# A second, transposed layout of the input for the first projection, with the normalisation moved

## The chip, the cores and the metric

The kernel runs on one core of one Trainium2 chip. The metric is the device time of one execution in microseconds (us); the median of a few runs is given. TensorE (PE in the profile) multiplies matrices into PSUM, VectorE (DVE) and ScalarE (ACT) do elementwise work from SBUF and PSUM, GpSimd (POOL) does elementwise work from SBUF and issues DMAs, SyncE (SP) issues DMAs. Each engine runs its own instructions in order and waits on semaphores for the others.

## The reference, cut to what matters

Two layers over 2048 tokens of width 1024: a Mamba-2 mixer and a latent attention mixer, each behind an RMS norm, and a last RMS norm. The part at issue is the first norm and the first projection:

```python
def rms_norm(x, g):
    y = xf * lax.rsqrt(jnp.mean(xf * xf, axis=-1, keepdims=True) + EPS)
    return y * g

hn = rms_norm(h, g_pre[0])                 # h is x, (2048, 1024)
proj = hn @ ssm_w_in                       # (1024, 5152)
z, xBC, dt_raw = split(proj)               # 2048, 3072, 32 columns
xBC = silu(causal_depthwise_conv(xBC, conv_w, conv_b))   # width 4, along the tokens
dt = softplus(dt_raw + dt_bias)
y = ssd_chunked_scan(...)                  # scan over 32 heads
y = group_norm(y * silu(z)) @ ssm_w_out    # added to the residual stream
```

The norm's factor r = rsqrt(mean(x^2) + EPS) is one number for each token. It may therefore be multiplied in before the projection or, since the projection is linear, on its result.

## The kernel before

Float32 accuracy is kept with pairs: each operand of a product is split into a rounded half (`hi`, by ScalarE) and the remainder (`lo`, by VectorE; `split`, lines 102 to 109), and each product is three matmuls (`mm3`, lines 80 to 84).

Layer 0 goes by blocks of 512 tokens (b = 0 to 3) and within a block by four groups of 8 heads (g). For each (b, g) there are these steps:

- `xbc` (line 283): B and C (two tiles of 128 channels) and then x (four tiles) of a group, channels on partitions, 512 tokens along the free axis; weights from `wunit`, loaded by SP and split. `evacuate` copies the PSUM bank to `craw` (ScalarE, L311), and makes the convolution (ScalarE L315, three times VectorE L317), tanh and product (L319, L320). `craw` has three buffers, PSUM's `mm` four.
- `zgate` (line 326): the gate z with tokens on partitions; `evacuate` takes tanh (L340) and a product (L341) straight from PSUM.
- `ssd` (line 438): the scan over four chunks of 128 tokens; GpSimd makes the remainders of some operands (`halves`, L455).
- `outp` (line 347): the output projection of the group, added to the residual rows `hs`.

Before a block's first group come `load_x` (line 255), which loads 512 rows of x, takes the mean square of each (ScalarE Square with accumulation, L155), the factor (`rsqrt`, a chain of ten small VectorE operations, lines 131 to 148) and multiplies the rows by it (L269); `prep` (line 271), which transposes the rows with 32 TensorE transposes of 128x128 (L163) into PSUM and splits them with the gain g0 into the eight tiles `xT` (L108 ScalarE, L109 VectorE; eight buffers, so a block's tiles take the places of the block before); and `steps` (line 375), the step sizes: 16 matmuls with `wdt` (L382), whose weights are split once at the start, then softplus on VectorE, then L422 to L424, whose result goes to DRAM (`cumT`) and comes back broadcast over the partitions (L471).

`mamba` (line 215) sets the order. Ahead of everything stand the first block's `load_x`, the constants, `prep`, `steps`, `xbc` and `zgate` of (0, 0). Then, item by item, the scan of (b, g) is woven with the output projection of the item before and the `xbc` and `zgate` of the next one; in group 2 of a block `load_x` of the next block is called at once, and `prep` and `steps` of it come last in the weave:

```python
            if g == G - 2 and b + 1 < NB:
                self.load_x(b + 1, self.a["x"][(b + 1) * TB:(b + 2) * TB])
                parts += [self.prep(b + 1, self.g0), self.steps(b + 1)]
```

The final order on each engine's queue is made by a scheduler from this order, priorities and its own estimates; tiles are places in pools with a fixed number of buffers, and a tile's first writer waits for the last reader of what lay there. After layer 0 come the second layer's projections (`mla`), attention and the output, which use `load_x` and `prep` too and are not changed.

Of the kernel before, what the change touches and what calls it, by code (L numbers as in the profile page):

```python
# [9 lines left out]
F32 = mybir.dt.float32  # L10
# [55 lines left out]
class Net:  # L66
# [50 lines left out]
    def wunit(self, src, n, scale=None, late=False):  # L117
        """Split weights; in the last layer's gates they take the place of the scan's states."""
# [12 lines left out]
    def rsqrt(self, pool, ms, n):  # L131
        """(ms + EPS) ** -0.5, elementwise on [P, n]."""
# [17 lines left out]
    def rows_rms(self, tiles, junk, width):  # L150
        """rsqrt(mean(x^2) + EPS) of each of the [P, width] tiles -> [P, len]."""
# [7 lines left out]
    def transposed(self, tiles, k, tag="tr"):  # L159
        """[P, k-th 128 columns] of four token tiles -> one PSUM bank [128 columns, 512 tokens]."""  # L160
        ps = self.t(self.pp, tag, [P, TB], bufs=4)
        for i, x in enumerate(tiles):
            self.nc.tensor.transpose(ps[:, i * P:(i + 1) * P], x[:, k * P:(k + 1) * P], self.ident)  # L163
        return ps

# [1 line left out]
    def constants(self, cp):  # L167
# [3 lines left out]
        # [lower triangle | hidden]  # L171
# [6 lines left out]
    def layer_constants(self, cp):  # L178
# [3 lines left out]
        wdt = self.t(self.wp, "wraw", [P, TB], bufs=WRAW)  # L182
        nc.sync.dma_start(wdt[:, :KD * H].rearrange("p (k c) -> p k c", k=KD),
                          a["ssm_w_in"][:, DI + 3072:].rearrange("(k p) c -> p k c", p=P))
# [7 lines left out]
        self.wdt = cp.tile([P, KD, 2, H], F32R, name="wdt")  # L192
        self.split(self.wdt[:, :, 0], self.wdt[:, :, 1], wdt[:, :KD * H].rearrange("p (k c) -> p k c", k=KD))
# [7 lines left out]
    # ---- layer 0: Mamba-2, by blocks of 512 tokens and groups of 8 heads;  # L201
# [13 lines left out]
    def mamba(self, cp):  # L215
        nc = self.nc
        self.state = [None] * G
# [36 lines left out]

    def load_x(self, b, src, tag="hx"):
        """A block's rows, normalised."""
# [14 lines left out]
    def prep(self, b, gain=None, tag="tr", each=4):  # L271
        """The normalised rows, channels on partitions, split."""
# [10 lines left out]
    def xbc(self, b, g):  # L283
        """B, C and x of a group: channels on partitions, convolution along the free axis, SiLU."""
        nc, w_in, xT = self.nc, self.a["ssm_w_in"], self.xT[b]
        outs = []
        for chans, tag, bufs in (([16 + g, 20 + g], "BC", 4), ([4 * g + j for j in range(4)], "xs", 8)):
# [19 lines left out]
            def evacuate(bank, i):  # L307
# [4 lines left out]
                nc.gpsimd.tensor_copy(self.halo[:, ch, :], raw[:, TB:TB + 3])  # L312
                acc = self.t(self.sp, "cacc", [P, TB], bufs=2)
                wk = [self.cw[:, 4 * ch + k:4 * ch + k + 1] for k in range(4)]
                nc.scalar.activation(acc, raw[:, 0:TB], AF.Identity, scale=wk[0], bias=self.cb[:, ch:ch + 1])  # L315
                for k in range(1, 4):
                    nc.vector.scalar_tensor_tensor(acc, raw[:, k:k + TB], wk[k], acc, ALU.mult, ALU.add)  # L317
                o = self.t(self.sp, tag, [P, TB], bufs=bufs)
                nc.scalar.activation(o, acc, AF.Tanh)  # L319
# [839 lines left out]
```

## Time and profile before

| | us |
|---|---|
| median of 3 runs | 3246.47 |
| lowest and highest run | 3245.31, 3246.8 |
| span of the profiled execution, first to last instruction | 3243.9 |
| TensorE busy in the span | 3194.4 |
| VectorE busy | 2589.0 |
| ScalarE busy | 2049.7 |
| GpSimd busy | 641.7 |

The profiled execution has no time of its own in the list of runs beside its span; what lies around the span is read from the difference to the median, 2.6 us. In the profile's rows L12 is line 12 of the kernel; a group's row has engine, operation, tiles written and read, sizes and count; a timeline row begins with the start and the duration; a row of the waits has the waiting instruction, what ended its wait, the sum, the count and the longest; a row of the stretches has the stretch, its length and the busy time of TensorE, the weight loads, VectorE, ScalarE and GpSimd, with instruction counts, then TensorE's granted clock, the share of the DMA engines and GB/s.

### The profile page before, as it was taken

To read this page: it belongs to the slowest core of one execution; us is meant where nothing else is said; L and a number is where in the kernel's file an instruction comes from. 1 tells how busy PE (TensorE), PEld (TensorE's weight loads), DVE (VectorE), ACT (ScalarE), POOL (GpSimd) and SP (SyncE) were. 2 spreads that over 40 slices of the span, in tenths; PEclk is the share of its full clock that TensorE was granted. 3 is DMA by queue.
4 is the path that set the end of the run, shared out by engine and by line. 5 is a ranking of instruction groups with operands and counts; after the bars stand their busy time and mean duration, and the time that the engine had idled before them with its cause. 6 is when DMAs were issued, how large, how long until landed. Compare 5 with 4: busy or idle time off the path is not lost. (4 is left out here: it accounts for less than half of the span.)

```text
span 3243.9 us, 50420 instructions
## 1 busy us (share of the span) xinstructions
PE 3194.4 (98%) x16704; PEld 2651.4 (82%) x16704; DVE 2589.0 (80%) x5480; ACT 2049.7 (63%) x5113; POOL 641.7 (20%) x854
## 2 busy tenths in 40 slices
PE   8999999999999999999999999999999999999998
PEld 6788888888888888888878888878888888887787
DVE  6888888888889888888777665678888888888665
ACT  5666666656657666666655554477777777777522
POOL 1221122221222212221111211322222222223100
PEclk9999999999999999999999999999999999999999
DMA  5333334333433344333476766954544445454385
GB/s 174 105 99 95 118 122 131 101 91 123 143 95 103 96 125 140 104 96 116 126 271 230 250 218 192 291 114 86 100 88 93 93 85 104 87 106 110 93 271 161
DMA packets 241397, 433.57 MB, mean 134 GB/s; under 512 B 26192, under 2 KB 100688, under 8 KB 239696
## 3 DMA queue, kind: packets, MB, share of 16 engines
q1 hardware_dynamic: 166704, 289.28, 29.4%
q0 software_dynamic: 74432, 141.06, 18.0%
q8 instruction: 132, 2.16, 0.3%
q14 instruction: 129, 1.06, 0.1%
HBM read 328.67 MB, written 101.58 MB: 133 GB/s over the span
## 5 line engine op out<-in xcount | busy, mean ns | idle before, releaser
L106 DVE TENSOR_TENSOR PTs<-tr,PTs 128x512 fp32r<-128x512 f32 (+2 forms) x576 | 359.9, 643 | 109.1 <-ACT PTs L105 106.4
L105 ACT ACTIVATE PTs<-tr 128x512 fp32r<-128x512 f32 (+2 forms) x576 | 314.2, 571 | 153.7 <-PE tr L901 152.4
L886 ACT ACTIVATE Pr<-mm,nm 128x512 f32<-128x512 f32 (+2 forms) x631 | 397.4, 641 | 20.2 <-DVE nm L878 20.2
L874 DVE TENSOR_REDUCE mx<-mm 128x1 f32<-128x512 f32 (+2 forms) x631 | 375.5, 608 | 33.0 <-PE mm L84 28.4
L105 ACT ACTIVATE wsp<-wraw 128x512 fp32r<-128x512 f32 (+1 forms) x452 | 251.8, 574 | 175.8 <-PE mm L84 88.4
L106 DVE TENSOR_TENSOR wsp<-wraw,wsp 128x512 fp32r<-128x512 f32 (+1 forms) x452 | 300.5, 678 | 70.0 <-ACT wsp L105 69.7
L82 PE MATMUL mm<-xT,wsp 128*128 128x512 f32 x800 | 324.4, 405 | 0.0
L901 PE MATMUL tr<-pack,Pr 128*128 128x128 f32 x2176 | 317.9, 273 | 2.6 <-ACT Os L923 2.4
L83 PE MATMUL mm<-xT,wsp 128*128 128x512 f32 x800 | 316.5, 396 | 0.0
L84 PE MATMUL mm<-xT,wsp 128*128 128x512 f32 x800 | 316.1, 395 | 0.0
L901 PEld LDWEIGHTS tr<-pack,Pr 128*128 128x128 f32 x2176 | 254.3, 141 | 40.9 <-ACT Os L923 2.9
L82 PE MATMUL mm<-K,xT 96*128 96x512 f32 (+2 forms) x639 | 248.6, 389 | 6.6 <-ACT Pr L886 5.2
L916 PE MATMUL tr<-PTs,xT 128*128 128x512 f32 (+2 forms) x576 | 253.9, 441 | 0.1
L82 PE MATMUL mm<-wsp,xT 128*128 128x512 f32 (+1 forms) x640 | 244.4, 382 | 0.0
L83 PE MATMUL mm<-wsp,xT 128*128 128x512 f32 (+1 forms) x640 | 240.0, 375 | 0.0
L84 PE MATMUL mm<-wsp,xT 128*128 128x512 f32 (+1 forms) x640 | 239.2, 375 | 0.0
L84 PE MATMUL mm<-K,xT 96*128 96x512 f32 (+2 forms) x639 | 231.5, 362 | 0.0
L317 DVE SCALAR_TENSOR_TENSOR cacc<-craw,pack,cacc 128x512 f32<-128x512 f32 x288 | 216.7, 774 | 18.4 <-ACT cacc L315 17.8
L83 PE MATMUL mm<-K,xT 96*128 96x512 f32 (+2 forms) x639 | 231.4, 362 | 0.0
L455 POOL TENSOR_TENSOR Xp<-Xw,Xp 128x512 fp32r<-128x512 f32 x64 | 83.0, 1298 | 708.1 <-ACT Xp L454 399.5
L497 ACT ACTIVATE Xw<-tr,d_wend 128x64 f32<-128x64 f32 x512 | 182.9, 358 | 55.4 <-DVE Xd L493 54.4
L917 PE MATMUL tr<-PTs,xT 128*128 128x512 f32 (+2 forms) x576 | 216.1, 377 | 0.0
(355 smaller groups left out, 8323.9 us busy)
## 6 DMA issues: line engine op xcount, KB each, us to landing
wraw<-in_ssm_w_in_dram SPq DMA_DIRECT2D x256, 256.0 KB, 2.8
big<-cumT SPq DMA_DIRECT2D x64, 512.0 KB, 4.2
wraw<-in_ssm_w_out_dram SPq DMA_DIRECT2D x128, 256.0 KB, 2.6
wraw<-in_ssm_w_in_dram SPq DMA_DIRECT2D x129, 128.0 KB, 2.2
xT<-qn_d POOLq DMA_DIRECT2D x64, 256.0 KB, 4.2
xT<-v_d POOLq DMA_DIRECT2D x32, 512.0 KB, 5.3
K<-kn_d POOLq DMA_DIRECT2D x15, 1024.0 KB, 9.2
wraw<-in_mla_w_uq_dram SPq DMA_DIRECT2D x36, 256.0 KB, 5.5
```

Source lines behind the costliest of these rows:

```text
L82: mm(out, l_hi, r_hi, start=start, stop=False)
L83: mm(out, l_hi, r_lo, start=False, stop=False)
L84: mm(out, l_lo, r_hi, start=False, stop=stop)
L105: nc.scalar.activation(hi, src, AF.Copy)
L106: nc.vector.tensor_tensor(lo, src, hi.bitcast(F32), ALU.subtract)
L317: nc.vector.scalar_tensor_tensor(acc, raw[:, k:k + TB], wk[k], acc, ALU.mult, ALU.add)
L497: act(Xw[:, hc], px[:, hc], AF.Copy, scale=wend[:, h0 + h:h0 + h + 1])
L874: v.tensor_reduce(mx[:, n:n + 1], s[:, :w], AX.X, ALU.max)
L886: nc.scalar.activation(x[:, :w], s[:, :w], AF.Exp, bias=nm, accum_out=sm[:, n:n + 1])
L901: nc.tensor.transpose(pt[:, j * P:(j + 1) * P], st["P"][j][kb], self.ident)
L916: nc.tensor.matmul(st["O"][:, c], vals[h, kb // 8][:, kb % 8, :], u[:, 0], start=kb == 0, stop=False)
L917: nc.tensor.matmul(st["O"][:, c], vals[h, kb // 8][:, kb % 8, :], u[:, 1], start=False, stop=kb == nk - 1)
```

## The change

The host hands the kernel the same input twice, as rows (`x`) and transposed (`xT`). The first projection's tiles are loaded from the transposed layout by SP, so layer 0's `prep`, and with it the transposes, is gone; the rows are still loaded, for r and, in block 0, as the residual rows.

- Block 0: `xT` is split as loaded, without r. The projection runs on it, and r is multiplied in afterwards: on each of the 24 channel tiles ahead of the convolution (VectorE, with r broadcast over the partitions, `rb`), on the 16 gate tiles in a new ScalarE copy (r by partition, `r0`), and on the step projection. The convolutions of the first B and C tiles are put off (`later`). `rb` is made by writing r to DRAM and reading it back broadcast, both from GpSimd's queue.
- Blocks 1 to 3: the rows are loaded early by GpSimd's queue, r is made in `load_xT` and broadcast the same way, and GpSimd multiplies each of the eight loaded tiles by `rb` before it is split. `load_xT` is a generator in the place of `prep`; its Squares are issued where the weave reaches it.
- The step weights are loaded and split anew in each block and use a weight buffer; the first block's `steps` comes after `xbc`.

The rest of the diff removes comments.

```diff
 def layer_constants
-        wdt = self.t(self.wp, "wraw", [P, TB], bufs=WRAW)
...
-        self.split(self.wdt[:, :, 0], self.wdt[:, :, 1], ...)
+        self.r0 = cp.tile([P, 4], F32, name="r0")
 def mamba
-        self.load_x(0, self.a["x"][0:TB])
+        rows, first = self.load_xT(0), self.xbc(0, 0)
+        next(rows)
         self.layer_constants(cp)
-        for part in (self.prep(0, self.g0), self.steps(0), self.xbc(0, 0), self.zgate(0, 0)):
+        for n in range(16):
+            next(rows, None)
+            next(first)
+            if n == 12:
+                while self.later:
+                    self.later.pop(0)()
+        for part in (first, self.steps(0), self.zgate(0, 0)):
...
             if g == G - 2 and b + 1 < NB:
-                self.load_x(b + 1, self.a["x"][(b + 1) * TB:(b + 2) * TB])
-                parts += [self.prep(b + 1, self.g0), self.steps(b + 1)]
+                parts += [self.load_xT(b + 1), self.steps(b + 1)]
+    def load_xT(self, b):
+        nc, v, t0 = self.nc, self.nc.vector, b * TB
+        rows = [self.a["x"][t0 + i * P:t0 + (i + 1) * P, :] for i in range(4)]
+
+        def norm(xs):
+            r = self.rows_rms(xs, [self.t(self.sp, "yt", [P, D], BF16, bufs=2) for _ in xs], D)
+            nc.gpsimd.dma_start(self.r_d[t0:t0 + TB].rearrange("(i p) -> p i", p=P), r)
+            rb = self.rb = self.t(self.hh, "rb", [P, TB], bufs=1)
+            self.behind = nc.gpsimd.dma_start(rb, self.r_d[t0:t0 + TB].partition_broadcast(P))
+            return r
+
+        self.xT[b] = []
+        if b:
+            xs = [self.t(self.hh, "hx", [P, D], bufs=4) for _ in range(4)]
+            with self.tc.issue_after(self.behind.ins):
+                for x, row in zip(xs, rows):
+                    nc.gpsimd.dma_start(x, row)
+            norm(xs)
+        for k in range(KD):
+            if k % 2 == 0:
+                pair = self.t(self.hh, "hx", [P, 2, TB], bufs=4)
+            x = pair[:, k % 2]
+            last = nc.sync.dma_start(x, self.a["xT"][k * P:(k + 1) * P, t0:t0 + TB])
+            if b:
+                nc.gpsimd.tensor_tensor(x, x, self.rb, ALU.mult)
+            elif k == 0:
+                yield
+            u = self.t(self.xq, "xT", [P, 2, TB], F32R, bufs=8)
+            self.split(u[:, 0, :], u[:, 1, :], x, self.g0[:, k:k + 1])
+            self.xT[b].append(u)
+            if k % 4 == 3 or b == 0 and k:
+                yield
+        if b == 0:
+            self.hs[0] = [self.t(self.hh, "hs", [P, D], bufs=4) for _ in range(4)]
+            for x, row in zip(self.hs[0], rows):
+                with self.tc.issue_after(last.ins):
+                    last = nc.sync.dma_start(x, row)
+                yield
+            v.tensor_copy(self.r0, norm(self.hs[0]))
+            yield
 def xbc, evacuate
+                def conv():
+                    if b == 0:
+                        nc.vector.tensor_tensor(raw[:, 3:], raw[:, 3:], self.rb, ALU.mult)
...
+                if b + g == 0 and tag == "BC":
+                    self.later.append(conv)
+                else:
+                    conv()
 def zgate, evacuate
+            if b == 0:
+                zn = self.t(self.sp, "craw", [P, TB], bufs=3)
+                nc.scalar.activation(zn, bank, AF.Copy, scale=self.r0[:, i:i + 1])
+                bank = zn
 def steps
+        raw = self.t(self.wp, "wraw", [P, TB], bufs=WRAW)[:, :KD * H]...
+        nc.sync.dma_start(raw, self.a["ssm_w_in"][:, DI + 3072:]...)
+        w = self.t(self.wp, "wsp", [P, 2, TB], F32R, bufs=WSP)[:, 0]...
+        self.split(w[:, :, 0], w[:, :, 1], raw)
...
-        nc.scalar.activation(rt, ps[0:2 * H, :], AF.Copy)
+        if b:
+            nc.scalar.activation(rt, ps[0:2 * H, :], AF.Copy)
+        else:
+            v.tensor_tensor(rt, ps[0:2 * H, :], self.rb[0:2 * H], ALU.mult)
 def layout
+        "xT": np.asarray(x)[0].T
```

More of the change, by code (lines that the diff above doesn't have):

```diff
@@ L191, in layer_constants @@
         nc.vector.memset(self.mk[:, P:], NEG)
-        self.wdt = cp.tile([P, KD, 2, H], F32R, name="wdt")
-        self.split(self.wdt[:, :, 0], self.wdt[:, :, 1], wdt[:, :KD * H].rearrange("p (k c) -> p k c", k=KD))
         nc.vector.tensor_scalar(self.cw, self.cw, 0.5, None, ALU.mult)
@@ L349, in outp @@
         nc, a, t0 = self.nc, self.a, b * TB
-        if g == 0:
+        if g == 0 and b:
             self.hs[b] = [self.t(self.hh, "hs", [P, D], bufs=4) for _ in range(4)]
@@ L377, in steps @@
         nc, v, xT = self.nc, self.nc.vector, self.xT[b]
+        raw = self.t(self.wp, "wraw", [P, TB], bufs=WRAW)[:, :KD * H].rearrange("p (k c) -> p k c", k=KD)
+        nc.sync.dma_start(raw, self.a["ssm_w_in"][:, DI + 3072:].rearrange("(k p) c -> p k c", p=P))
+        w = self.t(self.wp, "wsp", [P, 2, TB], F32R, bufs=WSP)[:, 0].rearrange("p (k n h) -> p k n h", k=KD, n=2)
+        self.split(w[:, :, 0], w[:, :, 1], raw)
         ps = self.t(self.pp, "tr", [P, TB], bufs=4)
@@ L381, in steps @@
             for n in range(2):
-                nc.tensor.matmul(ps[0:2 * H, :], self.wdt[:, k].rearrange("p n h -> p (n h)"), xT[k][:, n, :],
+                nc.tensor.matmul(ps[0:2 * H, :], w[:, k].rearrange("p n h -> p (n h)"), xT[k][:, n, :],
                                  start=k + n == 0, stop=k + n == KD)
@@ L1093, in run @@
             self.constants(cp)
+            self.r_d = dp.tile([T], F32, name="r_d")
             self.h_d = dp.tile([T, D], F32, name="h_d")
@@ L1131, in layout @@
     out = {
-        "x": np.asarray(x)[0], "positions": np.asarray(positions)[0],
+        "x": np.asarray(x)[0], "xT": np.asarray(x)[0].T, "positions": np.asarray(positions)[0],
         "c_pack": np.concatenate([pack[k] for k, _ in PACKED], axis=1),
```

24 lines of the change are left out of this document (11 added, 13 removed).

## The prediction

> **What bounds the kernel now.** I read the page's busy table first, then TensorE's waits, then the stretches.
>
> ```profile
> span 3243.9 us, 50420 instructions
> ...
> PE 3194.4 (98%) x16704; PEld 2651.4 (82%) x16704; DVE 2589.0 (80%) x5480; ACT 2049.7 (63%) x5113; POOL 641.7 (20%) x854
> ```
> ```profile
> PE tr L163 <- DMA wraw<-in_ssm_w_in_dram: 14.1, 1, 14.1
> ```
> ```profile
> 0.00:22.00 22.00, 7.94 (x39) 7.08 (x40) 11.07 (x43) 14.64 (x28) 0.64 (x7) 1.00 0.72 241
> ...
> 200.00:300.00 100.00, 100.00 (x488) 82.67 (x487) 85.85 (x178) 65.86 (x163) 19.73 (x24) 1.00 0.34 101
> ```
>
> TensorE has work in 98% of the span; 49.5 us are idle, and 14.1 of them are one wait, the start. In layer 0 (the second stretch; its columns are TensorE, weight load, VectorE, ScalarE, GpSimd) TensorE never rests and VectorE is at 86%. So the kernel is as long as TensorE's queue plus its holes: an instruction taken off TensorE is worth its place in the queue, an instruction on VectorE or GpSimd is free until TensorE reaches something that waits for it. The sums below are made on the profiled span, 3243.9 us. The median of the runs, 3246.47, is 2.6 above it for what lies around the span, which I leave alone. About 0.2% (6.5 us) is what a measurement here can tell from no change.
>
> **Removed: the transposes of blocks 1 to 3.** The PE timeline at the turn from block 0 to block 1:
>
> ```profile
> 346.66 0.39 PE L83 MATMUL mm<-wsp,xT 128*128 128x512 f32 x1
> 346.89 0.39 PE L84 MATMUL mm<-wsp,xT 128*128 128x512 f32 x1
> ...
> 351.04 0.60 PE L163 MATMUL tr<-pack,hx 128*128 128x128 f32 x4
> 351.39 0.48 PE L83 MATMUL mm<-wsp,yT 128*128 128x512 f32 x1
> 351.71 0.60 PE L163 MATMUL tr<-pack,hx 128*128 128x128 f32 x4
> ```
>
> One matmul of 512 columns takes 0.23 us of queue (346.66 to 346.89). Four transposes and one matmul take 351.71 - 351.04 = 0.67, so four transposes 0.44. A block has eight such fours, 3.5 us; three blocks 10.5 us. VectorE also loses the scaling of the rows (L269, four of 0.75 us a block, below), off the path. Block 0's 32 transposes are part of the start, next.
>
> **The start.**
>
> ```profile
> 14.06 3.78 PE L163 MATMUL tr<-pack,hx 128*128 128x128 f32 x16 [14.06 <-DMA wraw<-in_ssm_w_in_dram]
> 17.49 0.78 PE L82 MATMUL mm<-xT,wsp 128*128 128x512 f32 x1
> ...
> 21.70 3.87 PE L382 MATMUL tr<-xT,wdt 128*64 128x512 f32 x16
> ```
> ```profile
> 82.35 0.39 PE L82 MATMUL mm<-xT,wsp 128*128 128x512 f32 x1
> ```
> ```profile
> 10.34 0.21 DVE L194 TENSOR_SCALAR pack<-pack 128x96 f32<-128x96 f32 x1 [9.11 <-DMA pack<-in_c_pack_dram]
> ...
> 10.55 0.17 DVE L135 TENSOR_SCALAR rsx<-ms 128x4 f32<-128x4 f32 x1
> ...
> 13.46 0.16 DVE L146 SCALAR_TENSOR_TENSOR rsy<-rsq,rsy 128x4 f32<-128x4 f32 x1
> ```
>
> Today the constants land at 10.3 behind 2 MB of rows, the factor r is ready at 13.6, and the second group's first matmul starts at 82.35. In the changed program's order the constants follow 256 KB of x^T, and the first matmul needs only them, one weight tile and two splits: I put it at 7 us. TensorE starts cold (first matmul 0.78 us, not 0.39), which lasts some 6 us now and will again. From there to the second group it has 240 matmuls of 0.23 (56 us), the 16 step matmuls (3.8), some small ones (1) and about 3 us of cold: 70.8. But the convolutions of block 0 now wait for r in its broadcast form. The rows come after x^T, and two of their Squares stand behind the evacuations of the first two banks, which TensorE fills near 20 and 21 (48 matmuls, the first ones cold): the last Square ends near 24, r, with three weight splits between its links, is there near 29, and the broadcast (8.2 us, below) near 37. VectorE then has eleven operations for B and C before it goes on, and by its order the step chain reaches L486 some 1 to 3 us after TensorE does, with one wait before it (L453) of about 2. That makes 75, and a gain of 7.5 (3 to 11).
>
> **Block 0 behind the projection.**
>
> ```profile
> L320 DVE SCALAR_TENSOR_TENSOR xs<-xs,cacc 128x512 f32<-128x512 f32 x64 | 43.7, 685 | 0.7 <-ACT xs L319 0.7
> ```
>
> 24 channel tiles get one more VectorE multiplication. No row shows it; the nearest, with the same shape and both inputs in SBUF, takes 0.69: 16.4 us, mostly within 270 us where VectorE is 86% busy, so it goes to about 91%. The 16 gate tiles get a ScalarE copy (0.60, as the gate row below), 9.6 us on an engine with a third of its time free. Hidden as long as TensorE's next scan step isn't waiting; I charge 2 us (0 to 5). The step weights, split anew in each block (one 128 KB load, half a microsecond on each of two engines), are placed ahead of need and charged at nothing.
>
> **Blocks 1 to 3: the chain that takes the transposes' place.** This is the part that decides. Let t0 be the start of a block's last gate matmul plus 0.4. The rows of the next block are fetched early, but the changed program places the Squares between the gate evacuations, on ScalarE in this order: evacuation, Square, evacuation, Square.
>
> ```profile
> 347.32 0.60 ACT L340 ACTIVATE sz<-mm 128x512 f32<-128x512 f32 x1
> ```
> ```profile
> L269 DVE TENSOR_SCALAR hx<-hx,rsy x36: 348/747/754, 13.7 to 1793.1; 128x1024 f32<-128x1024 f32 x24, 128x256 f32<-128x256 f32 x12
> L155 ACT ACTIVATE yt<-hx x28: 1039/1042/1072, 4.1 to 1768.0; 128x1024 bf16<-128x1024 f32 x28
> L155 ACT ACTIVATION_READ_ACCUMULATOR yt<-hx x28: 185/186/217, 5.0 to 1769.0; 128x1 f32 x28
> ```
> ```profile
> L108 ACT ACTIVATE xT<-tr,pack x32: 677/688/703, 15.3 to 1141.1; 128x512 fp32r<-128x512 f32 x32
> L109 DVE SCALAR_TENSOR_TENSOR xT<-tr,pack,xT x32: 737/744/753, 16.8 to 1142.2; 128x512 fp32r<-128x512 f32 x32
> ```
> ```profile
> DMA to landing us min/median/max: 1.5/1.7/1.9
> ```
> ```profile
> xT<-qn_d POOLq DMA_DIRECT2D x64, 256.0 KB, 4.2
> ```
> ```profile
> DMA to landing us min/median/max: 2.2/5.6/9.9
> ```
>
> A Square with its read-out is 1.23 us, an evacuation 0.60 (and it starts right at t0 today). Stepping through the order, the last Square ends at t0 + 1.4 (t0 + 4.4 at the first turn, where the extra copies stand between). The r chain took 3.1 us at the start; here five larger VectorE operations of 0.6 to 0.75 stand between its links, so 6 us: r at +7.4 (first turn +9.1, as most of the five are done by then). GpSimd then sends r to DRAM and reads it back over 128 partitions, the second waiting for the first. Neither exists today. The landings above are a 64 KB write from SP (the cumulative decays), a 256 KB read from GpSimd, and everything on kr_d from GpSimd. Ends for the pair: 1.5 + 2.2 = 3.7 and 5.6 + 5.6 = 11.2; I take 4 + 4.2 = 8.2, near the middle, because the write goes out in 512 pieces of 4 bytes, finer than any row. [...]
>
> So the broadcast is there at t0 + 15.6 (+17.3 at the first turn). GpSimd multiplies eight tiles, and each is then split by ScalarE and VectorE:
>
> ```profile
> L455 POOL TENSOR_TENSOR Xp<-Xw,Xp x64: 1263/1296/1576, 90.9 to 1590.7; 128x512 fp32r<-128x512 f32 x64
> ```
> ```profile
> 264.59 1.29 POOL L455 TENSOR_TENSOR Xp<-Xw,Xp 128x512 fp32r<-128x512 f32 x1 [22.43 <-ACT Xp L454]
> ```
> ```profile
> 265.14 1.01 DVE L106 TENSOR_TENSOR wsp<-wraw,wsp 128x256 fp32r<-128x256 f32 x1 [0.25 <-ACT wsp L105]
> ...
> 274.60 0.43 DVE L106 TENSOR_TENSOR wsp<-wraw,wsp 128x256 fp32r<-128x256 f32 x1 [0.43 <-ACT wsp L105]
> ```
>
> Alone a product takes 1.26 to 1.30. But a VectorE split with both inputs in SBUF that meets a GpSimd product waits for its end: the one at 265.14 took 1.01 instead of 0.43 and ran on to 266.15, the product ended at 265.88. Until now these splits read PSUM; now they read the tile from SBUF, and each meets the next product. [...] Taking turns, a tile costs 1.26 + 0.65 = 1.9, and the last split ends 15.4 after the broadcast, at +31.0 (+32.7). Without the contention it would be 8 x 1.26 + 1.4 = 11.5, 3.9 less.
>
> TensorE's order decides what that costs. The step matmuls of the next block, which need these splits, now stand between output-projection matmuls: 52 matmuls and some transposes lie between t0 and the first of them, 24 more up to the last, so TensorE gets there at +18.9 if it never waits (first turn: 60 and 24, with half a microsecond for a weight split, +21.6). The wait is 31.0 - 18.9 = 12.1 at two turns and 32.7 - 21.6 = 11.1 at the first: 35.3 us. Behind it in TensorE's queue stand the rest of the output projection and the scan; VectorE and ScalarE stand in their own queues before the same splits, so weight splits and evacuations wait too; on GpSimd the scan's products are behind the eight and behind four DMAs that wait for the splits. All shift together, so I add nothing for them.
>
> **Sum.** -10.5 (transposes), -7.5 (start), +2 (block 0), +35.3 (waits) = +19.3, on the span 3263, on the median 3265.8; I say 3265.
>
> **Rivals.**
> - *Short chain.* [...] Chance 0.22, of which 0.14 within 0.2%.
> - *Chain hidden: faster.* The last split would have to be there at +18.9. That needs r in broadcast form 12.1 us earlier, before the last gate matmul; it decides from a Square placed about a group ahead, since the rows are there. Then -10.5 - 7.5 + 2 gives 3230. For it: TensorE has no wait at these turns now. Against it: the order of the Squares. Chance 0.10.
> - *Start eaten.* If VectorE's late convolutions of block 0 hold the first scan too, the start gives 0 and block 0 costs 5: 3276. Chance 0.10.
> - *Slow write.* The 4-byte pieces bring the pair to 11.2 or above: +3 a turn and at the start, 3277 and up. Chance 0.13.
>
> **How the numbers follow.** The forecast keeps 0.45, own range 3255 to 3274. Left out are the faster rival (0.10) and most of the slow write (0.10): range 3241 to 3280. Faster by over 0.2% (below 3240): 0.11; within 0.2%: 0.16; slower: 0.73.
>
> **What would show it.** Right: the first matmul near 7 us and the second group near 75; three waits of 10 us or so at the step matmuls, ended by ScalarE or VectorE splits of xT, whose own idle is ended by GpSimd; splits of xT longer than 0.75 us on VectorE. Wrong: PE without idle at the turns, or GpSimd's products ending before TensorE reaches the step matmuls; then the forecast falls to the faster rival.

## The result and the profile after

The changed kernel takes 3329.3 us (median of 4 runs, 3326.2 to 3333.1) where the kernel before takes 3245.9 in the same comparison: ratio 1.0249, 95% interval 1.0236 to 1.0261. It is slower, as forecast, but by 83 us instead of 19. Its profiled execution has a span of 3326.6 us.

The page of the changed kernel first. TensorE has 128 instructions fewer than before and is still busy 18 us longer, and its share falls from 98 to 97%:

```profile
span 3326.6 us, 50286 instructions
...
PE 3212.5 (97%) x16576; PEld 2650.2 (80%) x16576; DVE 2612.3 (79%) x5485; ACT 2060.4 (62%) x5127; POOL 699.5 (21%) x898
```

TensorE's waits in the changed kernel (engine, line, what ended the wait: us in all, times, longest). The first and third line are the step matmuls that wait for the splits of x^T. Of the other two the wait for a weight split (`wsp`) did not exist before, and the wait for y came to 1.0 us:

```profile
PE tr L443 <- ACT xT L108: 26.9, 3, 9.1
PE mm L84 <- DVE wsp L106: 13.2, 4, 4.6
PE tr L443 <- DVE xT L109: 9.2, 13, 0.8
...
PE tr L595 <- DVE y L590: 7.3, 4, 3.2
```

To see where the time went I set the same instruction of both programs side by side: the transposes of y for the third chunk of the last group but one of blocks 0, 1 and 2, shortly ahead of each turn. Before (the first fence) and after (the second), PE timeline:

```profile
323.94 0.60 PE L531 MATMUL tr<-pack,y 128*128 128x128 f32 x4
...
716.26 0.60 PE L531 MATMUL tr<-pack,y 128*128 128x128 f32 x4
...
1111.04 0.60 PE L531 MATMUL tr<-pack,y 128*128 128x128 f32 x4
```
```profile
333.30 0.60 PE L595 MATMUL tr<-pack,y 128*128 128x128 f32 x4
...
751.75 0.60 PE L595 MATMUL tr<-pack,y 128*128 128x128 f32 x4
...
1169.92 0.60 PE L595 MATMUL tr<-pack,y 128*128 128x128 f32 x4
```

The differences are +9.4, +35.5 and +58.9, and +82.7 at the end of the span. So start and block 0 cost 9.4 us (forecast: a gain of 5.5), and the three turns 26.1, 23.4 and 23.8 (forecast: 11.1 or 12.1 less the 3.5 of the transposes). With the 3.5 us of work that each turn saves, TensorE loses 29.6, 26.9 and 27.3 us at a turn. (The third figure holds all that follows, to the end of the span.)

**One turn in the trace.** TensorE at the first turn. Its last gate matmul starts at 356.26 (t0 is 356.7). It has come to the step matmuls at 371.87 and stands there for 8.94 us; the matmuls behind the wait start every 0.43 us instead of every 0.23; the last step matmul starts at 392.95, and three more waits follow within 50 us:

```profile
356.26 0.39 PE L84 MATMUL mm<-wsp,xT 128*128 128x512 f32 x1
...
371.48 0.39 PE L84 MATMUL mm<-wsp,yT 128*128 128x512 f32 x1
380.81 0.69 PE L443 MATMUL tr<-xT,wsp 128*64 128x512 f32 x1 [8.94 <-ACT xT L108]
381.30 0.63 PE L82 MATMUL mm<-wsp,yT 128*128 128x512 f32 x1
381.73 0.63 PE L83 MATMUL mm<-wsp,yT 128*128 128x512 f32 x1
...
392.95 0.44 PE L443 MATMUL tr<-xT,wsp 128*64 128x512 f32 x1
...
403.57 0.51 PE L82 MATMUL mm<-xT,wsp 128*128 128x512 f32 x1 [1.90 <-DVE hs L425]
...
411.72 0.49 PE L486 MATMUL tr<-big,pack 128*128 128x128 f32 x2 [1.61 <-DVE big L484]
...
440.87 2.07 PE L84 MATMUL mm<-xT,wsp 128*128 128x512 f32 x4 [3.90 <-DVE wsp L106]
```

GpSimd at the same turn. It writes r at 365.48, can issue the read only at 375.03, and starts the first product at 378.75:

```profile
365.48 0.80 POOL L265 DMA_DIRECT2D r_d<-rsy  x1 [1.25 <-DVE rss L142]
375.03 0.54 POOL L267 DMA_DIRECT2D rb<-r_d  x1 [8.75 <-DMA r_d<-rsy]
378.75 12.61 POOL L283 TENSOR_TENSOR hx<-hx,rb 128x512 f32<-128x512 f32 x8 [3.17 <-issue]
```

ScalarE's and VectorE's splits behind it come at a pitch of 1.69 us (382.95 to 384.64), and the last one ends at 392.89:

```profile
382.95 0.72 ACT L108 ACTIVATE xT<-hx,pack 128x512 fp32r<-128x512 f32 x1 [0.96 <-POOL hx L283]
384.64 0.72 ACT L108 ACTIVATE xT<-hx,pack 128x512 fp32r<-128x512 f32 x1 [0.96 <-POOL hx L283]
```
```profile
392.14 0.75 DVE L109 SCALAR_TENSOR_TENSOR xT<-hx,pack,xT 128x512 fp32r<-128x512 f32 x1 [0.24 <-ACT xT L108]
```

The same as stretches (their columns are TensorE, weight load, VectorE, ScalarE and GpSimd, then the granted clock). In the first TensorE does 25 instructions, 5.8 us of queue at 0.23, in 21 us; VectorE is half idle. In the second, which begins 42 us after the first ends, TensorE runs short again while VectorE is busy for 86% of the time:

```profile
372.00:393.00 21.00, 9.22 (x25) 4.62 (x25) 10.52 (x9) 6.29 (x10) 14.73 (x12) 0.76 0.15 32
...
435.00:447.00 12.00, 7.76 (x34) 6.72 (x35) 10.35 (x27) 8.29 (x26) 2.09 (x3) 0.74 0.22 67
```

VectorE's queue between the two stretches tells where the second comes from. VectorE stands 4.67 us in the step chain for ScalarE, which itself stands 6.54 us for a weight load (to 400.87). Then it is busy for 36.85 of the 40 us from 401.5 to 441.5. The weight split that TensorE waits 3.90 us for has no wait of its own ahead of it: it stands in that queue behind other work.

```profile
401.52 0.23 DVE L472 TENSOR_SCALAR big<-big 128x128 f32<-128x128 f32 x1 [4.67 <-ACT big L471]
...
440.13 1.28 DVE L106 TENSOR_TENSOR wsp<-wraw,wsp 128x512 fp32r<-128x512 f32 x2
```

A wait also costs beyond itself. In the two stretches above, with the waits of 8.94 and 3.90 us, the granted clock is 0.76 and 0.74, and the matmuls behind each wait start every 0.43 us. Behind the wait of 1.90 at 403.57 they start every 0.23 again; behind one of 1.98 at the second turn (822.02) they do so for 1 us and then start every 0.43 for 3 us. And behind a wait of 3.17 us in block 0, with TensorE busy ahead of it, four transposes take 0.92 instead of 0.60 and the next matmuls start every 0.43 too. So the trace shows no length from which a wait has this price.

```profile
147.10 0.92 PE L595 MATMUL tr<-pack,y 128*128 128x128 f32 x4 [3.17 <-DVE y L590]
```

**The start.** GpSimd, VectorE and TensorE in the changed kernel's first 85 us:

```profile
30.96 0.98 POOL L265 DMA_DIRECT2D r_d<-rsy  x1 [29.37 <-DVE r L297]
40.11 0.57 POOL L267 DMA_DIRECT2D rb<-r_d  x1 [8.16 <-DMA r_d<-rsy]
```
```profile
45.93 1.29 DVE L359 TENSOR_TENSOR craw<-craw,rb 128x512 f32<-128x512 f32 x2 [1.90 <-DMA rb<-r_d]
```
```profile
52.21 0.79 PE L82 MATMUL mm<-wsp,xT 128*128 128x512 f32 x1 [4.22 <-ACT craw L356]
...
61.15 0.69 PE L453 MATMUL tr<-pack,yt 64*128 64x64 f32 x4 [5.49 <-DVE yt L450]
...
84.68 0.39 PE L82 MATMUL mm<-xT,wsp 128*128 128x512 f32 x1
```

r is ready when GpSimd sends it, at 30.96, and lies on all partitions only at 45.9. Evacuations and the step chain wait for it, and TensorE for them, twice. The second group's first matmul starts at 84.68, 2.3 us later than before.

### The profile page after: what moved, and what is told of

It reads as the page before. It is cut to its first block, busy times and chain, and to the rows that moved or that the text cites. A ratio compares the mean times of both kernels' runs of the same rounds, so it can differ in the third digit from the quotient of the medians.

```text
span 3326.6 us, 50286 instructions
## 1 busy us (share of the span) xinstructions
PE 3212.5 (97%) x16576; PEld 2650.2 (80%) x16576; DVE 2612.3 (79%) x5485; ACT 2060.4 (62%) x5127; POOL 699.5 (21%) x898
## 4 chain that ended last, share of the span: by engine, by line
PE 52%; DVE 4%; DMA 3%; ACT 2%; issue 1%; POOL 0%; SPq 0%; ACTq 0%; DVEq 0%; POOLq 0%
PE mm L82 9%; PE mm L84 9%; PE mm L83 9%; PE tr L965 6%; PE tr L980 4%; PE tr L981 4%; PE tr L82 3%; PE tr L84 3%; PE tr L83 3%; DMA os<-ri_d 1%; PE tr L568 1%; DVE cacc L365 1%; DMA wraw<-in_mla_w_in_dram 1%; ACT PTs L105 1%; DMA wraw<-in_kv_w_up_dram 1%
## 5 line engine op out<-in xcount | busy, mean ns | idle before, releaser
L938 DVE TENSOR_REDUCE mx<-mm 128x1 f32<-128x512 f32 (+2 forms) x631 | 375.6, 608 | 35.3 <-PE mm L84 30.4
```

What stands on the lines that cost most here:

```text
L938: v.tensor_reduce(mx[:, n:n + 1], s[:, :w], AX.X, ALU.max)
```

## The experiments

All times stand beside the kernel before, run with them (3246.7 to 3247.9). "Lost" below is worked out from the PE timeline of each kernel: of every gap between two starts, what is over 0.23 us for a matmul of 512 columns (0.115 for 128, 0.107 for 64 columns), summed over a stretch; "up to the last step matmul" begins 25 us before the first of them, "behind" is the 80 us after the last. Overshoots of some 0.1 us, which every kernel has, are left out, so the figures hold to about 1 us; the kernel before loses some 1 us at most on either side.

I began with two theories. A: the chain's end sets the wait, and VectorE, 86% loaded, falls behind by as much and pays behind the turn. B: what stands behind the turn comes from the new order of the queues and not from the wait. The instructions of every engine are laid out anew when a part of the program is moved, so an edit changes more than the place of its own lines.

### One part alone: block 0, and its broadcast

Blocks 1 to 3 as before, block 0 as in the changed kernel (e2):

```
-                parts += [self.load_xT(b + 1), self.steps(b + 1)]
+                self.load_x(b + 1, self.a["x"][(b + 1) * TB:(b + 2) * TB])
+                parts += [self.prep(b + 1, self.g0), self.steps(b + 1)]
```

> Block 0 as in the changed kernel (x^T read directly, normalised behind the projection), blocks 1 to 3 as before (rows normalised by VectorE, transposed by TensorE). If the stages add up, as the traces read: +9.4 us for start and block 0, nothing at the turns: 3246 + 9.4 = 3255, between 3251 and 3260. If the prediction's start was right and the +9.4 comes from something that the later blocks do (their x^T loads, their products' DMAs): 3246 - 5.5 = 3240. If block 0's lag also reaches into the first turn: 3262 or more.

3257.1 us, ratio 1.0029 (1.0017 to 1.0041): the stages add up. Next the same with r broadcast on the chip (e20); `norm` then reads:

```
-            nc.gpsimd.dma_start(self.r_d[...], r)
+            diag = self.t(self.sp, "yt", [P, TB], bufs=2)
+            for i in range(4):
+                v.tensor_scalar(diag[:, i * P:(i + 1) * P], self.ident, r[:, i:i + 1], None, ALU.mult)
+            ps = self.t(self.pp, "tr", [P, TB], bufs=4)
+            nc.tensor.matmul(ps, self.ones, diag, start=True, stop=True)
             rb = self.rb = self.t(self.hh, "rb", [P, TB], bufs=1)
-            self.behind = nc.gpsimd.dma_start(rb, self.r_d[...].partition_broadcast(P))
+            self.behind = nc.scalar.activation(rb, ps, AF.Copy)
```

> As e2 (block 0 as in the changed kernel, blocks 1 to 3 as before), with block 0's r broadcast on the chip. In the traces the pair of DMAs took 15 us at the start and TensorE lost 25.6 us ahead of the first turn; with the on-chip broadcast it lost 15.9. If the DMA pair is what ate the start: 3257 - 10 = 3247, between 3243 and 3251. Rival (block 0's 24 multiplications on VectorE and the late convolutions eat it, whatever the broadcast): 3253 to 3258.

3247.9 us, ratio 0.9999 (0.9990 to 1.0008), as the first case expects. Of the waits of 4.2 and 5.5 us 1.4 are left, and the second group starts where the prediction had put it, at 75.5:

```profile
75.47 0.39 PE L82 MATMUL mm<-xT,wsp 128*128 128x512 f32 x1
...
135.90 1.09 PE L600 MATMUL tr<-pack,y 128*128 128x128 f32 x4 [3.14 <-DVE y L595]
...
323.20 0.60 PE L600 MATMUL tr<-pack,y 128*128 128x128 f32 x4
```

From 6.9 us ahead of the kernel before at 75.5 it falls back to 0.7 us ahead at 323.2 (before: 82.35 and 323.94). So block 0 behind the projection costs 6 us even then, half of it in one wait for y (with the slow clock behind it: four transposes in 1.09).

### The turn's chain: broadcast, product, place

On-chip broadcast (as above) in the changed kernel, all four blocks (e3):

> The changed kernel with r broadcast on the chip instead of through DRAM: four VectorE multiplications of the identity by r's columns, one TensorE matmul with ones, one ScalarE copy; no DMA. In all four blocks. Theory A: the pair of DMAs took 13.3 us at the first turn and 15.0 at the start; the new way takes about 3. First split at t0 + 14 instead of + 24, TensorE arrives at + 15.4, and the splits' pitch of 1.69 us brings the last to about + 26: a wait of some 5 us a turn instead of 16.8, and behind it a backlog in proportion, 2 to 4 instead of 10 to 13; at the start r in broadcast form at 34 instead of 46, so the waits of 4.2 and 5.5 us in block 0 go. Time 3329 - 10 - 3 x 19 = 3262, between 3250 and 3275. Theory B (the part behind doesn't depend on the wait): 3329 - 10 - 3 x 11 = 3286, between 3278 and 3294.

3282.3 us, ratio 1.0105 (1.0090 to 1.0120): by the total theory B. Per turn 8.3, 7.7 and 7.8 us are lost up to the last step matmul (changed kernel: 15.4, 15.6, 15.6), so the wait was halved; behind it 9.2, 8.6 and 8.6 stay (changed kernel: 14.3, 13.3, 9.7).

The changed kernel with the products on VectorE instead (e4):

```
-                nc.gpsimd.tensor_tensor(x, x, self.rb, ALU.mult)
+                v.tensor_tensor(x, x, self.rb, ALU.mult)
```

> The changed kernel with the eight products of blocks 1 to 3 on VectorE instead of GpSimd, in the same place. Theory A (start of the chain decides, and VectorE's backlog behind it): a tile costs 0.69 + 0.74 = 1.43 instead of the 1.69 that the trace shows with the two engines taking turns, 2 us a turn less for the last split, but VectorE has 5.5 us more work there, which it pays behind the turn: 3322 to 3333. Rival (the two engines' contention on GpSimd's product is what costs the turns): the wait falls by most of the 8 x 0.97 that splits idle in each turn and its backlog by as much: 3285 to 3305.

3313.1 us, ratio 1.0202 (1.0185 to 1.0219): between the two cases. 10.5 to 11.1 us are lost up to the last step matmul, 6.5 to 15.5 behind. Taking the products off GpSimd is worth some 5 us of each wait, more than theory A gave it. Whether it is the contention or VectorE's shorter product (0.69 us, where GpSimd's takes 1.26 at the shortest) isn't told apart by this run.

The changed kernel with norm placed ahead of the last group's gate projection, blocks 1 to 3 (e1):

```
             norm(xs)
+            yield
 ...
-                parts += [self.load_xT(b + 1), self.steps(b + 1)]
+                rows = self.load_xT(b + 1)
+                parts.insert(-1, itertools.islice(rows, 1))
+                parts += [rows, self.steps(b + 1)]
```

> The changed kernel, with one thing moved: for blocks 1 to 3 the Squares, r and its way to DRAM and back (norm) are placed ahead of the last group's gate projection instead of behind it; products, splits and step matmuls stay where they are. Theory A (the chain and the backlog it leaves): the gate sweep is 96 matmuls of 0.23 us and scan work, some 30 us or more, which is longer than the 24 us from the last gate matmul to the first split in the changed kernel's trace. So the three waits at the step matmuls (16.8 us a turn, with the cold clock) fall to under 3, and what stands behind them (10 to 13 us a turn: the waits for a weight split, for y and for hs) goes with them. Block 0 keeps its +9.4. Time 3246 + 9.4 - 10.5 + at most 9: 3245 to 3255. Theory B (what stands behind comes from the changed order and queues, not from the wait): the step waits go, the rest stays: 3329 - 3 x 16 = 3281, between 3272 and 3290.

3303.1 us, ratio 1.0167 (1.0147 to 1.0187): both cases miss. Up to the last step matmul 16.9, 13.6 and 13.9 are lost, hardly less, and behind it only 6.3, 2.6 and 3.7. The second turn on GpSimd and TensorE:

```profile
765.82 0.79 POOL L268 DMA_DIRECT2D r_d<-rsy  x1 [5.69 <-DVE rsy L147]
768.04 1.28 POOL L523 TENSOR_TENSOR Xp<-Xw,Xp 128x512 fp32r<-128x512 f32 x1 [1.43 <-ACT Xp L522]
775.52 0.55 POOL L270 DMA_DIRECT2D rb<-r_d  x1 [6.21 <-DMA r_d<-rsy]
...
779.00 12.15 POOL L287 TENSOR_TENSOR hx<-hx,rb 128x512 f32<-128x512 f32 x8 [1.23 <-issue]
```
```profile
781.07 0.64 PE L447 MATMUL tr<-xT,wsp 128*64 128x512 f32 x1 [5.10 <-ACT xT L109]
```

The Squares end at 751.5, but with convolutions laid out between its links the r chain takes 14 us, GpSimd's queue takes scan products in between, and the step matmuls have moved forward too. So the chain still ends last. And a loss of 13.6 us ahead of the last step matmul leaves 2.6 behind it here, where 7.7 left 8.6 with the on-chip broadcast: what stands behind doesn't follow the length of the wait. Theory A falls for that part. I went on with theory O, stated in the next expectations: the chain's end sets the wait, the layout sets what stands behind.

Early norm and on-chip broadcast together (e5), then the same with block 0 as before (e7):

> Both earlier changes together: for blocks 1 to 3 norm stands ahead of the last group's gate projection, and r is broadcast on the chip in all blocks. Theory O (the wait at the step matmuls is set by the end of the chain Squares - r - broadcast - products; what stands behind the turn is set by the order in which VectorE's weight splits and convolutions were laid out, not by the length of the wait): with the early placement the trace showed r at 765.4 and the first step matmul asked for at 776.0; without the DRAM pair the broadcast is there near 769, the products run 770 to 783, TensorE waits 2 to 4 us a turn, and behind it stand 3 to 6 as with the early placement alone. Start and block 0 as with the on-chip broadcast, some 8 us less than in the changed kernel. Time 3303 - 8 - 3 x 10 = 3265, between 3255 and 3275. Rival (the splits' pitch of 1.69 us keeps the wait at 8 a turn, as on-chip alone): 3275 to 3285.

> Block 0 as before (rows normalised by VectorE, transposed by TensorE; no multiplication behind the projection), blocks 1 to 3 with x^T read directly, norm placed early and r broadcast on the chip. If the stages add up: e5's turns and before's start, which by the traces is 0 to 3 us worse than the start with the on-chip broadcast: e5 + 0 to 4. If block 0's start was what makes the turns dear (its order pushes the others): e5 - 5 or less.

3267.8 us, ratio 1.0062 (1.0045 to 1.0079), and 3271.9 us, 1.0073 (1.0058 to 1.0088): both as theory O has it in the total, but the losses lie elsewhere than I put them. Behind the turns some 2.3 to 3 are left; ahead of the last step matmul 7.7 to 10.0, and there TensorE waits for the scan. GpSimd and TensorE with both edits, second turn:

```profile
743.02 12.31 POOL L291 TENSOR_TENSOR hx<-hx,rb 128x512 f32<-128x512 f32 x8 [5.92 <-ACT rb L274]
...
755.88 1.28 POOL L527 TENSOR_TENSOR Xp<-Xw,Xp 128x512 fp32r<-128x512 f32 x1
```
```profile
757.21 0.80 PE L84 MATMUL tr<-Xp,Bt 128*128 128x512 f32 x1 [3.87 <-POOL Xp L527]
```

The scan's low half Xp stands behind eight products in a row on GpSimd. I had not counted that wait for any of these kernels.

### The step matmuls later

The changed kernel with the step matmuls and the step chain moved behind the next block's first x projection (e6; the scan needs them a group later):

```
+                if g == G - 1:
+                    parts.insert(-1, self.steps(b + 1))
 ...
-                parts += [self.load_xT(b + 1), self.steps(b + 1)]
+                parts += [self.load_xT(b + 1)]
```

> The changed kernel with one thing moved: for blocks 1 to 3 the step matmuls and the step chain stand between the next block's first x projection and its gate projection, instead of right behind the gate projection of the last group but one. The scan needs their results only one group later. Squares, broadcast through DRAM, products and splits stay. Theory O: TensorE's first use of a split is then the B/C sweep, 96 output-projection matmuls (22 us) and scan work later, some 35 us behind the last gate matmul; the first split is there at + 24 and each sweep step takes 1.4 us against a pitch of 1.69. The waits at the turns fall from 16 to 0 to 3, with an order that is laid out anew: 3246 + 9 - 10.5 + 0 to 15 = 3245 to 3260. Rival (VectorE is too full: the chain, wherever it stands, holds VectorE's queue and TensorE waits for weight splits instead): 3270 to 3290.

3320.5 us, ratio 1.0222 (1.0207 to 1.0238): wrong by 60 us. TensorE waits once a turn, 16 to 19 us, for ScalarE: at the first turn for a weight split, at the others for the scan's Xp. ScalarE and TensorE at the first turn:

```profile
378.58 0.72 ACT L108 ACTIVATE xT<-hx,pack 128x512 fp32r<-128x512 f32 x1 [11.54 <-POOL hx L286]
...
390.84 0.72 ACT L108 ACTIVATE wsp<-wraw,pack 128x512 fp32r<-128x512 f32 x1
```
```profile
391.61 2.07 PE L82 MATMUL mm<-wsp,yT 128*128 128x512 f32 x4 [16.24 <-ACT wsp L108]
```

The eight splits of x^T stand in ScalarE's queue and wait for GpSimd there; the weight split stands behind them and is done right after the last. So the step matmuls were only the first to meet the chain: the splits themselves block. Around the step chain, now late, 2.5 to 3.5 us are lost, behind a wait longer than any in the changed kernel. And from the end of that wait on, 90 us lose 4.4, 5.1 and 4.1 us by the same count, the slow matmuls right behind it (four in 2.07 at the first turn) among them, where the changed kernel loses 14.3, 13.3 and 9.7 behind its last step matmul. So with this as the only edit most of what stood behind the turn is gone, and the wait itself has grown.

The same late place with early norm, on-chip broadcast and block 0 as before (e10):

> As the one with block 0 as before, early norm and the broadcast on the chip, and the step matmuls placed late too. Everything that TensorE meets at the turn is then finished ahead. Theory O: no waits at the turns over 1 us; what is left is the removal of the 96 transposes of blocks 1 to 3 (10.5 us) less a few us of new waits: 3236 to 3243, faster than the kernel before. Rival (GpSimd's products and VectorE's splits contend wherever they stand, each split held for a product's end, and VectorE is full): 3250 to 3265.

3277.9 us, ratio 1.0088 (1.0073 to 1.0103): above the rival's range too, and no better than e7. The waits are for Xp again, 2.3 to 2.9 us twice a turn.

### GpSimd relieved, norm earlier

As e7 with the products on VectorE (e13); then norm at the start of the group (`next(rows)` ahead of the output projection instead of the `insert`; e14):

> As e7 (block 0 as before; blocks 1 to 3 with x^T, norm ahead of the gate projection, r broadcast on the chip), with the eight products of a block on VectorE instead of GpSimd. Theory Q (with r there in time, what is left at a turn is GpSimd's queue: eight products in a row, each split held for a product's end, and the scan's low halves behind them; e7's trace has waits of 3.2 to 3.9 us for Xp by GpSimd and 8 us lost up to the last step matmul, 2.5 behind): the loss falls from 10.5 to 3 or 4 a turn, 3272 - 3 x 7 = 3251, between 3245 and 3257. Rival (VectorE is full: the products' 5.5 us a block come back as waits for VectorE): 3262 to 3275.

> As e13, with norm moved further ahead, to where the kernel before has its Squares in program order: ahead of the output projection of the last group but one, a group before the splits. Nothing of the chain but the product and the split is then left near the turn. Theory Q: losses of 1 to 3 us a turn; without the 96 transposes (10.5 us) and with the twelve matmuls and copies of the broadcast (some 5 us in all) 3246 - 10.5 + 5 + 3 = 3243, between 3238 and 3250. Rival (placement was enough in e13): the same as e13.

3264.2 us, ratio 1.0056 (1.0041 to 1.0072), and 3263.8 us, 1.0050 (1.0038 to 1.0063). The rivals hold: relieving GpSimd brought 8 us and not 21, and the earlier norm nothing. But it moved the loss. With norm at the group's start, nothing at all is lost up to the last step matmul, and all of it stands behind, 7.2 to 8.6 a turn, in one wait of 5.0 to 6.3 us and, for the other 2.2 to 2.3, the slow matmuls after it. TensorE's waits (the fourth, of 2.5, is at the start):

```profile
PE tr L486 <- DVE big L484: 20.1, 4, 6.3
```

So the step chain on VectorE is late by itself, with no wait ahead of it.

Norm at the group's start in the changed kernel alone, with DRAM and GpSimd kept (e16); and e14's edits with the changed kernel's block 0 (e17):

> The changed kernel with norm moved alone: for blocks 2 and 3 to the start of the group (ahead of its output projection), for block 1 ahead of the gate projection as in e1, because block 0's convolutions still need the one buffer of the broadcast r. The way through DRAM and GpSimd's products stay. Theory Q: r is there long before the last gate matmul, so the DMA pair (13 us) is hidden at turns 2 and 3; GpSimd's products and the splits' pitch stay as in e5, 8 to 10 us a turn with 2.5 behind, against 16 to 18 in e1: 3303 - 2 x 6 = 3291, between 3284 and 3298. Rival (the prediction's faster case: once r is early the whole chain is hidden): 3303 - 2 x 16 = 3271 or less.

> The changed kernel's block 0 (x^T read directly, normalised behind the projection) with r broadcast on the chip, products on VectorE, norm at the start of the group for blocks 2 and 3 and ahead of the gate projection for block 1. If the stages add up: e14's turns 2 and 3, e13's turn 1, and a start that by the on-chip trace is some 2 us better than before's: e14 + 0 to 3, between 3238 and 3250. If block 0's 24 multiplications on VectorE cost more than the start brings: 3250 to 3260.

3305.3 us, ratio 1.0175 (1.0161 to 1.0189), and 3264.2 us, 1.0050 (1.0037 to 1.0062): both worse than expected. With DRAM and GpSimd kept, r is early at turns 2 and 3 and the step matmuls don't wait; TensorE waits 9.3 and 10.1 us for Xp, behind seven products, and 6.6 and 6.2 us for the step chain:

```profile
696.71 8.61 POOL L290 TENSOR_TENSOR hx<-hx,rb 128x512 f32<-128x512 f32 x7 [4.12 <-DMA wraw<-in_ssm_w_in_dram]
```

### All of them together

Block 0 as before, norm at the group's start, broadcast on the chip, products on VectorE, step chain late (e18); beside it the same with the changed kernel's block 0 (e19), and e18 with the broadcast through DRAM (e21):

> As e14 (block 0 as before; blocks 1 to 3 with x^T, norm a group ahead, broadcast on the chip, products on VectorE), with the step matmuls and the step chain placed late as in e6. In e14's trace the only loss left at a turn is the wait for the step chain at L486, 5.0, 6.3 and 6.3 us and the slow matmuls after it, 8 us a turn; in e6 the late place had 2.5 to 3.5 us instead. If what stood behind the turns was the place of the step chain: 3264 - 3 x 6 = 3246, and with the 10.5 us of the transposes showing fully down to 3238. Rival (VectorE, with its products added, is full and pays at another place): 3255 to 3265.

> As e17 (block 0 as in the changed kernel with r broadcast on the chip), with the step matmuls and chain late. If the stages add up: e18 plus 0 to 8, the difference being the first turn, where norm stands only ahead of the gate projection (e17 lost 8 there up to the last step matmul and 6 behind).

> As e18, with r broadcast through DRAM by GpSimd again, a group ahead of its use. It saves TensorE the two broadcast passes of 1.1 us and the 0.8 us wait ahead of them in each of three blocks (8 us), and VectorE and ScalarE five small operations; but GpSimd stands some 9 us for its own write, and the scan's low halves stand behind that. If GpSimd's time is free there: e18 - 8. If the scan's halves wait: e18 + 0 to 10.

3242.5 us, ratio 0.9988 (0.9979 to 0.9997): within the range of the first case, and level with the kernel before or a hair faster. The 0.12% is less than the 0.2% that the prediction took for what a measurement here can tell, and less than half of the 10.5 us that the transposes take. The late place took 21 us off, and the losses behind the step matmuls fell from 7.2, 8.6 and 8.6 to 1.7, 1.6 and 1.8. With the changed kernel's block 0 3250.6, 1.0014 (1.0005 to 1.0023), 8 us more, as expected. With DRAM 3258.9, 1.0037 (1.0024 to 1.0049): 16 us more, above my range. TensorE then waits 4.2 to 4.4 us a block for hs, ahead of the turn. It does so through VectorE's queue: the first product stands there 10.11 us for the broadcast r, and the operation on hs stands behind the product. VectorE, then TensorE, in block 2:

```profile
1071.30 0.69 DVE L284 TENSOR_TENSOR hx<-hx,rb 128x512 f32<-128x512 f32 x1 [10.11 <-DMA rb<-r_d]
1071.91 0.74 DVE L424 SCALAR_TENSOR_TENSOR hs<-mm,rr,hs 128x512 f32<-128x512 f32 x1
```
```profile
1072.71 0.79 PE L83 MATMUL mm<-wsp,yT 128*128 128x512 f32 x1 [4.35 <-DVE hs L424]
```

So the pair of DMAs, 14.3 us here (the write is sent at 1056.97), isn't hidden by an early norm: the products have moved forward in VectorE's queue too, and VectorE asks for the broadcast r 4.2 us after the write is sent.

## Why the prediction was wrong

+19.3 was forecast and +82.7 measured on the span. The sign was right, and so was the mechanism of the wait at the step matmuls: the three waits of some 9 us were there, ended by the splits of x^T, which waited for GpSimd's products and had themselves grown on VectorE (0.74 to 1.44 us). Two things failed: the pair of DMAs was priced too low, at the start and at the turns, and the step that put nothing behind the turns was wrong. By the prediction's own steps:

- **Transposes, -10.5.** Not measured by themselves. TensorE has 16576 instructions instead of 16704, the 128 that were to go.
- **Start, -7.5.** First matmul at 7.40 (forecast 7) and r at 31.0 (29) were right. The broadcast was forecast for 37 and came at 45.9: the pair of DMAs took 15.0 us (30.96 to 45.93), not 8.2. With it on the chip the second group starts at 75.47, the forecast 75; with it through DRAM at 84.68. The term was +2.3 instead of -7.5, and the DMA pair accounts for 9.2 of the difference of 9.8 (84.68 against 75.47).
- **Block 0, +2 (0 to 5).** +7.0 (from +2.3 to +9.4), outside its range. The 6 us in the run with the on-chip broadcast show that it isn't the DMA; 3.2 us are the wait for y at 147.10. Its product with the gate (L590) stands in VectorE's queue behind two of block 0's new multiplications and six convolution operations, and the term had those multiplications as mostly hidden.
- **The chain at a turn, +35.3.** Measured 15.4 + 15.6 + 15.6 = 46.6. At the first turn GpSimd sends r at t0 + 8.8 (forecast 9.1) and starts the first product at + 22.1 (17.3): the pair of DMAs again, 13.3 us instead of 8.2. That was the rival of the slow write, to which I gave 0.13 and +3 a turn. Products and splits took 14.1 us, not 15.4 (a pitch of 1.69, not 1.9), so that the last split ended at + 36.2 and not + 32.7; and the slow clock behind a wait of 9 us (0.76 in that stretch) was in no term.
- **"All shift together, so I add nothing for them."** This, about what stands behind the wait, is the step that failed worst: 14.3 + 13.3 + 9.7 = 37.3 us. The engines don't shift together, and what each meets behind the turn isn't set by how long it stood. Losses up to the last step matmul and behind, per turn: changed kernel 15.5 and 12.4, on-chip broadcast 7.9 and 8.8, early norm 14.8 and 4.2, both 8.8 and 2.4, norm at the group's start with products on VectorE 0 and 8.1, and with the chain late 0 and 1.7. The step chain of 25 VectorE operations, set right behind the turn, and the weight splits and convolutions laid out around it fill VectorE's queue, and TensorE meets it there: at the first turn 1.61 us for the chain itself and 3.90 for a weight split, each of the other two 4.6 for a weight split, and slow matmuls (every 0.43 us) behind the long ones. That most of it goes when the chain is placed late is shown twice, with that as the only edit (12.4 a turn to 4.5, behind a longer wait) and in the last version (8.1 to 1.7). The early norm takes much of it away too (4.2), so the chain's place isn't the only thing that sets it. How it divides between the chain and what is laid out around it is not shown, because every edit lays the queues out anew.

These corrections, +9.8, +5.0, +11.3 and +37.3, with +19.3 make 82.7. The sum agrees better than its parts: turn by turn the two losses add up to 29.7, 28.9 and 25.3, where the transposes of y gave 29.6, 26.9 and 27.3.

Of the rivals, the slow write was true but priced too low (+3 at the start and a turn, where the pair took 6.8 and 5.1 more than forecast) and without what stands behind it. "Short chain" (no contention, and perhaps a quick DMA pair) didn't come: the contention was there (a pitch of 1.69), and a quick pair, on which its 0.14 within 0.2% leaned, is shown by no run; in the changed kernel the pair took 13.0 to 15.0 us. "Chain hidden" was wrong in its condition: it said that a Square placed a group ahead decides, and with only that moved, at two of the three turns, the time was 3305, because GpSimd's products then held the scan and the step chain came late. "Start eaten" was true too (+2.3 and +7.0, where it had 0 and +5). I had given them as alternatives to the forecast; they came on top of it.

## What to carry to other kernels

A piece of work taken off the bounding engine is worth its place in the queue only if nothing that replaces it can stand at the head of another in-order queue: count what is behind it on every engine that it passes, not only who needs its result. Here eight products on GpSimd held up weight splits on ScalarE and scan halves on GpSimd that needed nothing from them. Bound a transfer in 4-byte pieces far above any contiguous row of the trace (here 8.6 to 9.0 us for 2 KB, where a 64 KB write took 1.7), and where a long dependent chain stands right behind a wait, price the chain's own place too.

## What was unexpected

A write of 2 KB in 512 pieces of 4 bytes took up to 9.0 us from issue to landing (8.6 at the shortest), and the read behind it 3.6 to 5.8. The line is the answer for the tensor r_d in the changed kernel, the four writes and the four reads together:

```profile
DMA to landing us min/median/max: 3.6/7.2/9.0
```

Beside VectorE's splits of x^T GpSimd's product itself grew from 1.26 to 1.73 us and the split from 0.74 to 1.44 (min, median, max in ns of both groups), so that a tile took 1.69 us where 1.26 and 0.74 one after the other would take 2.0:

```profile
L283 POOL TENSOR_TENSOR hx<-hx,rb x24: 1257/1725/1747, 378.7 to 1224.6; 128x512 f32<-128x512 f32 x24
...
L109 DVE SCALAR_TENSOR_TENSOR xT<-hx,pack,xT x32: 744/1440/1455, 7.4 to 1227.1; 128x512 fp32r<-128x512 f32 x32
```
